# A two-layer diffusion backbone on one core: the context's output projection behind the last tokens, its norm last

## The chip, the cores and the metric

The kernel runs on one core of a Trainium2 chip. The time is the device time of one execution, in microseconds; three runs of the kernel before are given. The engines are PE (TensorE, the matmuls; its weight loads are listed as PEld), DVE (VectorE), ACT (ScalarE), POOL (GpSimd) and SP (SyncE, which issues most of the DMA). Each takes its instructions strictly in the order in which they were placed on it, and they wait for each other by semaphores.

## The reference

Two layers over 1024 latent tokens of width 1024, with 256 context tokens that have the same weights and a conditioning of their own. Cut to what the change touches:

```python
for i in range(2):
    h_lat = rms_norm(x_lat, norm_g[i]) * (1 + sc_l) + sh_l
    h_ctx = rms_norm(x_ctx, norm_g[i]) * (1 + sc_c) + sh_c
    # layer 0: two kinds of attention, heads gated by silu, then @ w_out, for latent and context
    # layer 1: convolution module and neighbourhood attention, for latent tokens only;
    #          of the context it uses keys and values (h_ctx @ w_in)
    x_lat = x_lat + g_l * y_lat
    if i == 0:
        x_ctx = x_ctx + g_c * y_ctx
return rms_norm(x_lat, final_g)
```

Between the layers, then, each token's row of `x` gets the output projection of layer 0 added, is normalised by its root mean square, scaled and shifted, and is the input of layer 1's projections.

## The kernel before

All numbers are float32. A matmul on full precision is made of three: both operands are split into a rounded part (`hh`, `wh`) and the rest (`hl`, `wl`), and `mm3` adds hi·hi, hi·lo and lo·hi into one bank. ScalarE rounds (line 312) and GpSimd or VectorE subtracts (line 315).

Tokens are worked on in three chunks: c = 0 is the context (256 tokens), c = 1 the first 512 latent tokens, c = 2 the last 512. Activations lie transposed: 128 partitions of the width by the tokens of the chunk, eight such tiles (e or dk, 0 to 7).

The program is written as generators that yield between steps. `weave` runs the attention's steps and, after each so many of them, some steps of a second generator as a filling. That gives a program order. The sequence on each engine is then made by a scheduler, which simulates the program with time estimates of its own and prefers what comes earlier in the program order; `tc.issue_after(x)` forbids it to place what is written inside ahead of instruction x. Nothing at run time changes the sequence.

The end of layer 0 is this:

- The attention's last groups: scores (lines 509, 513), exponentials on ScalarE (521), splitting into `ph` and `pl` (312, 315), weighted sums of the values in the bank `ov` (460 to 462), and then, on VectorE, the division by the sum of weights (470 to 473, 670) and the gate (672). Two sets of `ov` follow one another in the same bank.
- `final_proj(c)`: the last quarter of layer 0's output projection for chunk c. For each e, six matmuls (two weight tiles, three each) into a bank `po`, then on VectorE `x += g * po` (line 954), then on ScalarE the square of `x` (979 for the first, 985 after), and an addition of the square to a running sum (987), on GpSimd or VectorE; for the context by odd and even e. For the context and chunk 1 the squares have one buffer, so a square waits until the one before has been added. Chunks 1 and 2 also store `x` to memory; the context doesn't.
- `norm_h(c)`: `rstd_steps` sums the squares over partitions by matmuls with ones (259, `trs`), adds the epsilon (262, `rbv`), raises to the power -1/2 on GpSimd (246), refines by a Newton step on VectorE (247 to 249, `nt`, `nr`), and, two yields later, spreads the result over the partitions by matmuls with the identity (269, `bc`). `make_h` then multiplies all eight tiles on VectorE (322), shifts on ScalarE (325 or 328) and splits (312; 315 on GpSimd or 326 on VectorE).

In the kernel before, the filling of the attention's last steps is: projection of chunk 1, its norm, projection of the context, its norm. Projection and norm of chunk 2 follow when the attention is done. Layer 1 starts with `conv_proj`: value (first product `p`), gate (second) and a third, of other weights (`od_cs`), for chunk 1 and then for chunk 2; then the convolution on VectorE (1083, 1085) while further projections run on TensorE. At the very end a final norm is made for pieces of the tokens by the same `rstd_steps`; its squares are added on lines 1442 and 1445, and its multiplies are on GpSimd (1458, from a copy of the broadcast made on line 1453) and VectorE (1460).

Of the kernel before, what the change touches and what calls it, by code (L numbers as in the profile page):

```python
# [18 lines left out]
P = 128  # L19
# [49 lines left out]
NFILL = (39, 39, 36)  # L69
GL = 12  # L70
HV = 'gggvvvvg'
O1 = (6, 65, 41, 14)
TICK0, TICK1 = (1, 3)
PLAN = 'p0mmnbwmm1h2nbhnbh'
MWR = "ABxAVx"
# [13 lines left out]
def tile_kernel(ctx: ExitStack, tc: tile.TileContext, a, out):  # L89
    nc = tc.nc  # L90
    VE, SC, GP, PE, SY = nc.vector, nc.scalar, nc.gpsimd, nc.tensor, nc.sync
# [12 lines left out]
    def bank(tag, name):  # L104
        if tag == "pp" and solo[0]:
            turn[0] += 1
            tag = ("pp", "mx")[turn[0] // 2 % 2]
        return ps.tile([P, 512], F32, tag=tag, name=name, bufs=BUFS[tag])
# [3 lines left out]
    def nm(s):  # L112
        uid[0] += 1
        return f"{s}_{uid[0]}"
# [17 lines left out]
    ones = cp.tile([P, 2], F32, tag="ones", name="ones")  # L132
# [109 lines left out]
    def newton_rsqrt(pool, v, n, tag):  # L242

        r = pool.tile([P, 16], F32, tag=tag + "r", name=nm("nr"), bufs=2)
        t = pool.tile([P, 16], F32, tag=tag + "t", name=nm("nt"), bufs=2)
        GP.tensor_tensor(r[:, :n], v, mhalf[:, :n], op=ALU.pow)
        VE.tensor_tensor(t[:, :n], r[:, :n], v, op=ALU.mult)
        VE.scalar_tensor_tensor(t[:, :n], t[:, :n], -0.5, r[:, :n], op0=ALU.mult, op1=ALU.mult)
        VE.scalar_tensor_tensor(r[:, :n], t[:, :n], 1.5, r[:, :n], op0=ALU.add, op1=ALU.mult)
        return r  # L250

    def rstd_steps(pool, accs, n, tag, inv=1.0, tr="tr"):


        nb = n // P
        tr = bank(tr, nm("trs"))
        for b in range(nb):
            for k, acc in enumerate(accs):
                PE.matmul(tr[:, 2 * b : 2 * b + 2], acc[:, b * P : (b + 1) * P], ones, start=(k == 0),
                          stop=(k == len(accs) - 1))  # L260
        v = pool.tile([P, 8], F32, tag="rbv", name=nm("rbv"), bufs=2)
        VE.tensor_scalar(v[:, :nb], tr[:, 0 : 2 * nb].rearrange("p (b two) -> p b two", two=2)[:, :, 0],
                         inv, EPS, op0=ALU.mult, op1=ALU.add)
        r = newton_rsqrt(pool, v[:, :nb], nb, "rb")
        yield
        yield
        bc = bank(tag, nm("bc"))
        for b in range(nb):
            PE.matmul(bc[:, b * P : (b + 1) * P], r[:, b : b + 1].broadcast_to([P, P]), ident, start=True, stop=True)
        return bc  # L270
# [9 lines left out]
    def run(gen):  # L280

        while True:
            try:
                next(gen)
            except StopIteration as e:
                return e.value


    def new_h(c):
        if c == 0:  # L290
            t = bigp.tile([P, 2, DK, 256], F32R, tag="big", name=nm("hc"))
            return (t[:, 0], t[:, 1])
        th = bigp.tile([P, DK, 512], F32R, tag="big", name=nm("hh"))
        tl = bigp.tile([P, DK, 512], F32R, tag="big", name=nm("hl"))
        return (th, tl)
# [32 lines left out]
                SC.activation(x, x, AF.Identity, bias=shift)  # L328
                split(x, h[0][:, dk, :], h[1][:, dk, :])

    def mm3(o, lh, ll, rh, rl, first, last):
        PE.matmul(o, lh, rh, start=first, stop=False)  # L332
        PE.matmul(o, lh, rl, start=False, stop=False)  # L333
        PE.matmul(o, ll, rh, start=False, stop=last)  # L334

    def w_tiles(pool, n, width, bufs, rb):

# [355 lines left out]
    with ExitStack() as p0x:  # L693
# [6 lines left out]
        with tc.tile_pool(name="st0", bufs=1, reuse_waits="tile") as st0:  # L700
# [36 lines left out]
            accs, bcs, mh = [], [], [(0, 0), (0, 1), (1, 0), (1, 1)]  # L737
# [180 lines left out]
    with tc.tile_pool(name="o0", bufs=1, reuse_waits="tile") as op_:  # L918
# [26 lines left out]
        def out0(fs, e, c, wh, wl):  # L945
            n = CHUNKS[c][1]
            es = slice(e % 2 * P, (e % 2 + 1) * P)
            cond = 1 if c == 0 else 0
            pp = bank("pp", nm("po"))
            for f in fs:  # L950
                mm3(pp[:, :n], wh[f][:, es], wl[f][:, es], oh[c][0][:, f, :], oh[c][1][:, f, :], f == fs[0], f == fs[-1])
                if f % 2 == 1:
                    yield
            VE.scalar_tensor_tensor(x1[c][:, e, :], pp[:, :n], modT[0][:, 16 + e, cond : cond + 1], x1[c][:, e, :],  # L954
                                    op0=ALU.mult, op1=ALU.add)

        def out0_part(fs):
            for e2 in range(4):
                w = load_w(op_, a["ev_wo"], e2, 256, WO, dks=fs, rb=2)
                if fs == parts[0]:  # L960
                    load_x1(e2)
                for e in (2 * e2, 2 * e2 + 1):
                    for c in range(3):
                        yield from out0(fs, e, c, *w)

        accs = {}

        def final_proj(c):

            t0, n = CHUNKS[c]  # L970
            na = 2 if c == 2 else 1
            pool, tag, bufs = (kvp, "QH", 3) if c == 2 else (op_, "acc1", 1)
            accs[c] = [pool.tile([P, 512], F32, tag=tag, name=nm("acc1"), bufs=bufs)[:, :n] for _ in range(na)]
            for e in range(DK):
                yield from out0(final, e, c, *ws[e // 2])
                if c > 0:
                    SY.dma_start(X1[:, e, t0 - 256 : t0 - 256 + n], x1[c][:, e, :])
                if e < na:
                    SC.activation(accs[c][e], x1[c][:, e, :], AF.Square)
                else:  # L980
                    if c < 2:
                        sq = op_.tile([P, 512], F32, tag="sq1", name=nm("sq1"), bufs=1)
                    else:
                        sq = kvp.tile([P, 512], F32, tag="QL", name=nm("sq1"), bufs=3)
                    SC.activation(sq[:, :n], x1[c][:, e, :], AF.Square)
                    k = e % na if e < 7 else 0
                    (GP if (k if c == 2 else e % 2) else VE).tensor_tensor(accs[c][k], accs[c][k], sq[:, :n], op=ALU.add)

        def norm_h(c):

            n = CHUNKS[c][1]
            bc = yield from rstd_steps(op_, accs[c], n, "pp", tr="pp")
            h1[c] = new_h(c)
            make_h(1, c, lambda dk: x1[c][:, dk, :], bc[:, :n], h1[c])
            yield

        weave(main, O1[0], load_oh(parts[0]), 6, False)
        weave(main, O1[1], out0_part(parts[0]), 48, False)
        weave(main, O1[2], chain(load_oh(parts[1]), out0_part(parts[1])), 30, False)
        ws = [load_w(op_, a["ev_wo"], e2, 256, WO, "gv"[e2 % 2], dks=final, rb=2) for e2 in range(4)]  # L1000
        fill = chain(final_proj(1), norm_h(1), final_proj(0), norm_h(0))
        weave(main, NSTEP[U1 // 2] - GL - O1[0] - O1[1] - O1[2], fill, O1[3])
        solo[0] = True
        run(final_proj(2))
        run(norm_h(2))
    a0x.close()


# [606 lines left out]
```

## Time and profile before

| | |
|---|---|
| three runs | 1559.18, 1565.87, 1557.75 us (median 1559.18) |
| profiled execution | 1559.91 us; its span 1558.1 us; mean granted clock 0.965 |
| TensorE busy | 1459.1 us, 94% |
| VectorE busy | 1050.0 us, 67% |
| GpSimd busy | 801.5 us, 51% |
| ScalarE busy | 746.9 us, 48% |

The page sums the busy time of each engine over the whole span; a view of windows gives the same for any stretch, with the clock that TensorE was granted there (1.00 is full). A list of groups gives count, busy time, mean duration, and the idle time ahead of such instructions with what ended it. A timeline gives single instructions: start, busy time, engine, line, operation, and in brackets the idle time before them.

### The profile page before, as it was taken

Reading aid. Unit: us, or ns where it says so; the run is one execution under the profiler, and the core shown is the slowest. Engines: PE = TensorE matmul, PEld = TensorE weight load, DVE = VectorE, ACT = ScalarE, POOL = GpSimd, SP = SyncE. Lnnn points to the kernel's source line nnn. Section 1 sums busy time; section 2 is a strip of 40 time slices with the busy share of each in tenths; the row PEclk is TensorE's granted clock in tenths of the full one; section 3 lists DMA queues with packets and bytes.
Section 4 is the critical chain, followed back from the end, with each engine's and each line's share of the span. In section 5 each row is a group of like instructions: output and inputs, shape, how many; then the busy total and the mean of one; then the engine's idle time right before and its main releaser. Section 6 shows DMA issues by size and latency. Waiting matters only on the chain.

```text
span 1558.1 us, 21469 instructions
## 1 busy us (share of the span) xinstructions
PE 1459.1 (94%) x7084; PEld 1175.6 (75%) x7084; DVE 1050.0 (67%) x2113; ACT 746.9 (48%) x1418; POOL 801.5 (51%) x637
## 2 busy tenths in 40 slices
PE   6899999998998989999999878999999899989995
PEld 2786978896896768876866657888887688868875
DVE  2833557579579765466677846999756566577866
ACT  3721434444435564447556663443334355455563
POOL 3530434455445765557656664665632344364675
PEclk9899999999999999999999889999999899999996
DMA  9473315422312245121112012111445777878632
GB/s 366 161 244 124 108 57 181 143 70 92 119 51 79 92 151 177 54 68 50 51 31 92 7 34 86 58 55 41 142 159 192 216 204 236 263 227 243 183 111 108
DMA packets 154168, 199.83 MB, mean 128 GB/s; under 512 B 14716, under 2 KB 95816, under 8 KB 154056
## 3 DMA queue, kind: packets, MB, share of 16 engines
q1 hardware_dynamic: 147392, 186.88, 38.0%
q10 hardware_dynamic: 6664, 11.57, 2.3%
q8 instruction: 56, 0.92, 0.2%
q14 instruction: 56, 0.46, 0.1%
HBM read 148.07 MB, written 49.02 MB: 126 GB/s over the span
## 4 chain that ended last, share of the span: by engine, by line
PE 79%; DVE 13%; DMA 3%; issue 2%; ACT 2%; POOL 1%; SPq 0%; DVEq 0%; POOLq 0%; ACTq 0%
PE p L332 7%; PE p L333 7%; PE p L334 7%; PE ov L460 4%; PE ov L462 4%; PE ov L461 4%; PE st L509 4%; PE st L513 4%; PE po L333 4%; PE po L332 4%; PE po L334 4%; PE pq L332 3%; PE pq L334 3%; PE pq L333 3%; PE pm L184 2%
## 5 line engine op out<-in xcount | busy, mean ns | idle before, releaser
L315 POOL TENSOR_TENSOR pl<-pf,ph 128x512 fp32r<-128x512 f32 (+4 forms) x321 | 396.8, 1247 | 375.8 <-ACT ph L312 328.7
L521 ACT ACTIVATE pf<-st 128x512 f32<-128x512 f32 x284 | 166.3, 597 | 210.3 <-PE st L513 171.0
L315 POOL TENSOR_TENSOR wl<-wr,wh 128x512 fp32r<-128x512 f32 (+2 forms) x131 | 170.5, 1313 | 141.4 <-ACT wh L312 121.4
L312 ACT CAST ph<-pf 128x512 fp32r<-128x512 f32 (+4 forms) x364 | 209.2, 588 | 29.0 <-PE ov L461 16.7
L332 PE MATMUL p<-hh,wh 128*128 128x512 f32 x448 | 178.2, 398 | 5.3 <-ACT hh L312 2.8
L333 PE MATMUL p<-hl,wh 128*128 128x512 f32 x448 | 176.1, 394 | 0.6 <-POOL hl L315 0.6
L334 PE MATMUL p<-hh,wl 128*128 128x512 f32 x448 | 173.7, 394 | 0.0
L509 PE MATMUL st<-QH,KAt 128*128 128x512 f32 (+4 forms) x364 | 140.9, 388 | 8.9 <-ACT pf L521 8.1
L460 PE MATMUL ov<-ph,Vt 128*128 128x512 f32 (+4 forms) x364 | 142.5, 392 | 5.6 <-DVE y L670 4.3
L462 PE MATMUL ov<-pl,Vt 128*128 128x512 f32 (+4 forms) x364 | 141.9, 390 | 1.8 <-POOL pl L315 1.8
L461 PE MATMUL ov<-ph,Vt 128*64 128x512 f32 (+4 forms) x364 | 140.5, 386 | 0.0
L513 PE MATMUL st<-QL,KBt 68*128 68x512 f32 (+4 forms) x364 | 136.4, 386 | 2.0 <-DVE QL L438 2.0
L1085 DVE SCALAR_TENSOR_TENSOR cps<-U,taps,cps 128x512 f32<-128x512 f32 x184 | 126.4, 751 | 0.9
L312 ACT CAST wh<-wr 128x512 fp32r<-128x512 f32 (+2 forms) x134 | 81.2, 613 | 92.3 <-DMA wr<-in_od_d_dram 19.1
L332 PEld LDWEIGHTS p<-hh,wh 128*128 128x128 f32 x448 | 85.1, 190 | 23.8 <-ACT hh L312 3.0
L333 PEld LDWEIGHTS p<-hl,wh 128*128 128x128 f32 x448 | 85.2, 190 | 18.7 <-POOL hl L315 1.7
L334 PEld LDWEIGHTS p<-hh,wl 128*128 128x128 f32 x448 | 85.1, 190 | 17.5
L633 DVE TENSOR_REDUCE mp<-mx 128x1 f32<-128x512 f32 x128 | 85.2, 681 | 17.4 <-PE mx L632 16.5
L332 PE MATMUL pq<-wh,hh 128*128 128x384 f32 x256 | 88.4, 345 | 2.8 <-ACT hh L312 2.8
L509 PEld LDWEIGHTS st<-QH,KAt 128*128 128x128 f32 x364 | 69.7, 192 | 26.5 <-ACT pf L521 11.9
L954 DVE SCALAR_TENSOR_TENSOR x<-po,modT,x 128x512 f32<-128x512 f32 (+1 forms) x72 | 47.0, 657 | 62.1 <-PE po L334 61.7
L333 PE MATMUL pq<-wl,hh 128*128 128x384 f32 x256 | 87.4, 342 | 0.0
(280 smaller groups left out, 3470.8 us busy)
## 6 DMA issues: line engine op xcount, KB each, us to landing
mw<-in_mod_w_dram SPq DMA_DIRECT2D x16, 1024.0 KB, 5.5
Q<-qs SPq DMA_DIRECT2D x40, 256.0 KB, 2.2
QH<-Q SPq DMA_DIRECT2D x80, 128.0 KB, 2.7
mw<-in_mod_w_dram SPq DMA_DIRECT2D x16, 512.0 KB, 6.7
wr<-in_od_d_dram SPq DMA_DIRECT2D x32, 256.0 KB, 3.2
wr<-in_ev_qkv_dram SPq DMA_DIRECT2D x16, 384.0 KB, 5.2
KAt<-KD SPq DMA_DIRECT2D x16, 384.0 KB, 5.9
wr<-in_od_wo_dram SPq DMA_DIRECT2D x22, 256.0 KB, 3.3
```

The costliest lines, as they stand in the source:

```text
L312: acts.append(SC.copy(hi, src))
L315: (GP if leng == "g" else VE).tensor_tensor(lo, src, hi.bitcast(F32), op=ALU.subtract)
L332: PE.matmul(o, lh, rh, start=first, stop=False)
L333: PE.matmul(o, lh, rl, start=False, stop=False)
L334: PE.matmul(o, ll, rh, start=False, stop=last)
L460: PE.matmul(o, V[:, 64:192], ph[:, :n], start=(t == 0), stop=False)
L461: PE.matmul(g.ov[0:64, q0 : q0 + n], V[:, 0:64], ph[:, :n], start=False, stop=False)
L462: PE.matmul(o, V[:, 64:192], pl[:, :n], start=False, stop=(last and g.sink is None))
L509: sts.append(PE.matmul(st[:, :n], KA[:, cs], g.QH[:, q0 : q0 + n], start=True, stop=False))
L513: PE.matmul(st[:, :n], KB[0:68, cs], g.QL[0:68, q0 : q0 + n], start=False, stop=True)
L521: acts.append(SC.activation(pf[:, :n], st[:, :n], AF.Exp, scale=1.0 if g.bias else SCALE))
L1085: VE.scalar_tensor_tensor(pc, uc, w, pc, op0=ALU.mult, op1=ALU.add)
```

## The change

Five places are edited: the number 14 in `O1`, which says how many steps of the filling go with the attention's last steps, is 11; a list `last` collects the last matmul of every `mm3` and the matmuls of `rstd_steps` (the parameter `last` of `mm3` is renamed `end`); the context's projection and norm are taken out of the filling; and behind the projection of chunk 2 they are written out by hand. `pinned(gen, k)` runs k steps of a generator such that nothing in them is placed ahead of the latest matmul in `last`. The order by hand: four steps of the context's projection (four e), the sums of chunk 2's norm, the other four e, broadcast and making of chunk 2's `h`, and then the context's norm. What is computed is the same.

```diff
-O1 = (6, 65, 41, 14)
+O1 = (6, 65, 41, 11)
...
+    last = []
+
     def rstd_steps(pool, accs, n, tag, inv=1.0, tr="tr"):
...
-                PE.matmul(tr[:, 2 * b : 2 * b + 2], acc[:, b * P : (b + 1) * P], ones, start=(k == 0),
-                          stop=(k == len(accs) - 1))
+                last.append(PE.matmul(tr[:, 2 * b : 2 * b + 2], acc[:, b * P : (b + 1) * P], ones, start=(k == 0),
+                                      stop=(k == len(accs) - 1)))
...
-    def mm3(o, lh, ll, rh, rl, first, last):
+    def mm3(o, lh, ll, rh, rl, first, end):
         PE.matmul(o, lh, rh, start=first, stop=False)
         PE.matmul(o, lh, rl, start=False, stop=False)
-        PE.matmul(o, ll, rh, start=False, stop=last)
+        last.append(PE.matmul(o, ll, rh, start=False, stop=end))
...
-        fill = chain(final_proj(1), norm_h(1), final_proj(0), norm_h(0))
+        fill = chain(final_proj(1), norm_h(1))
         weave(main, NSTEP[U1 // 2] - GL - O1[0] - O1[1] - O1[2], fill, O1[3])
         solo[0] = True
         run(final_proj(2))
-        run(norm_h(2))
+        f0, n2 = final_proj(0), norm_h(2)
+
+        def pinned(gen, k):
+            with tc.issue_after(last[-1].ins):
+                for _ in range(k):
+                    next(gen, None)
+
+        pinned(f0, 4)
+        pinned(n2, 1)
+        pinned(f0, 5)
+        next(n2)
+        pinned(n2, 2)
+        run(norm_h(0))
```

In the changed kernel line numbers from 261 on are 2 higher, and from the end of layer 0 on 14 higher.

On TensorE the context's matmuls leave the attention's last steps and come in two halves around the sums of chunk 2. Here is the changed kernel's TensorE where the projection of chunk 2 ends and layer 1 begins (`po` are banks of the projection, `hc` the context's operand, `hh` the latent tokens', `trs` and `bc` sums and broadcast of a norm, `p_2417` the value, `p_2418` the gate):

```order
L336 MATMUL po_9362<-hh_7170,wl_8824 128x512
L334 MATMUL po_9375<-hc_7129,wh_8805 128x256
...
L336 MATMUL po_9406<-hc_7129,wl_8812 128x256
L261 MATMUL trs_9413<-ones,acc_2347_9280 128x2
...
L334 MATMUL po_9434<-hc_7129,wh_8817 128x256
...
L271 MATMUL bc_9478<-ident,nr_9424 128x128 x4
L334 MATMUL p_2417_9654<-hh_9225,wh_9607 128x512
...
L261 MATMUL trs_9513<-ones,acc_2363_9374 128x2 x2
L334 MATMUL p_2418_9679<-hh_9225,wh_9607 128x512
```

Before, the sums of chunk 2 came behind the product `p` that is first here, and its broadcast behind the second; now the first comes behind the broadcast, and 24 context matmuls stand on each side of the sums.

On VectorE, the division of the last but one set of weighted sums (`ov`, reciprocal `r`, quotient `y`) stood among the context's norm before (`x_1769` is the context's `x`):

```order
L249 SCALAR_TENSOR_TENSOR nr_9356<-nt_9357,nr_9356 128x2
L322 SCALAR_TENSOR_TENSOR x_1769_7130<-x_1769_7130,gs_105,bc_9362 128x256 x8
L470 STREAM_TRANSPOSE r_2306_9123<-ov_8931 64x256 x2
L326 SCALAR_TENSOR_TENSOR hc_9365<-x_1769_7130,modT_103,hc_9365 128x256
L472 RECIPROCAL r_2307_9124<-r_2306_9123 128x8
L326 SCALAR_TENSOR_TENSOR hc_9365<-x_1769_7130,modT_103,hc_9365 128x256
L473 STREAM_TRANSPOSE rb_9125<-r_2307_9124 128x256
L670 TENSOR_TENSOR y_9130<-ov_8931,rb_9125 64x256 x2
```

and now stands alone:

```order
L317 TENSOR_TENSOR pl_8989<-pf_8990,ph_8988 128x512
L472 STREAM_TRANSPOSE r_2299_9093<-ov_8931 64x256 x2
L474 RECIPROCAL r_2300_9094<-r_2299_9093 128x8
L475 STREAM_TRANSPOSE rb_9095<-r_2300_9094 128x256
L672 TENSOR_TENSOR y_9100<-ov_8931,rb_9095 64x256 x2
```

The context's norm is now on VectorE behind chunk 2's, ahead of the first instruction of the convolution.

The scheduler also sorts some steps of layer 1 anew, though nothing is edited there. The place that the prediction speaks of is GpSimd at the end of the program (`sq` are squares of the final norm, `nr_15684` and `nr_15779` the powers of its last two pieces, `bcs` the copied broadcasts). Before:

```order
L1442 TENSOR_TENSOR sq_3810_15698<-sq_3810_15698,sq_3822_15744 128x256
L246 TENSOR_TENSOR nr_15684<-rbv_15682,mhalf 128x2
L246 TENSOR_TENSOR nr_15779<-rbv_15777,mhalf 128x2
L1458 TENSOR_TENSOR x_3242_13685<-x_3242_13685,bcs_15756 128x256 x4
L1458 TENSOR_TENSOR x_3242_13685<-x_3242_13685,bcs_15788 128x256
```

Now:

```order
L246 TENSOR_TENSOR nr_15684<-rbv_15682,mhalf 128x2
L1456 TENSOR_TENSOR sq_3810_15698<-sq_3810_15698,sq_3822_15744 128x256
L1472 TENSOR_TENSOR x_3242_13685<-x_3242_13685,bcs_15756 128x256 x4
L246 TENSOR_TENSOR nr_15779<-rbv_15777,mhalf 128x2
L1472 TENSOR_TENSOR x_3242_13685<-x_3242_13685,bcs_15788 128x256
```

The last piece's power has four multiplies of the piece before it ahead of it. Its broadcast on TensorE is still the last one.

## The prediction

> **What bounds the kernel now.** I read the shares and the chain of waits first, then windows around the change, then groups and single instructions in them.
>
> ```profile
> span 1558.1 us, 21469 instructions
> PE 1459.1 (94%) x7084; PEld 1175.6 (75%) x7084; DVE 1050.0 (67%) x2113; ACT 746.9 (48%) x1418; POOL 801.5 (51%) x637
> PE 79%; DVE 13%; DMA 3%; issue 2%; ACT 2%; POOL 1%; SPq 0%; DVEq 0%; POOLq 0%; ACTq 0%
> ```
>
> TensorE is busy 94% of the span and makes 79% of the chain: an edit pays only where TensorE idles or runs at a lower clock. The change touches 869 to 967 us, so here is that stretch by stage: second-last attention group (869 to 892), last group (892 to 907), the handover to its weighted sums (907 to 911), these sums (911 to 924), their division (924 to 927), the projection of the last tokens (927 to 941), layer 1's first projection (941 to 954), and the wait for its second token chunk (954 to 967). The columns are TensorE, its weight loads, VectorE, ScalarE and GpSimd busy, the granted clock, and DMA. The last row, from a second query, is a sample of the convolution that follows.
>
> ```profile
> 869.00:892.00 23.00, 19.30 (x103) 13.88 (x100) 22.69 (x38) 16.37 (x32) 18.22 (x14) 1.00 0.00 1
> 892.00:907.00 15.00, 12.42 (x53) 8.25 (x53) 10.81 (x21) 11.40 (x25) 10.92 (x11) 1.00 0.03 9
> 907.00:911.00 4.00, 0.92 (x3) 0.51 (x4) 3.87 (x9) 3.55 (x9) 3.71 (x4) 0.79 0.00 0
> 911.00:924.00 13.00, 12.18 (x40) 8.16 (x40) 2.88 (x6) 8.35 (x15) 8.74 (x8) 0.80 0.11 40
> 924.00:927.00 3.00, 0.00 (x0) 0.00 (x0) 2.46 (x7) 0.34 (x2) 0.00 (x0) 0.90 0.00 0
> 927.00:941.00 14.00, 13.88 (x49) 11.18 (x50) 7.46 (x10) 6.22 (x12) 7.73 (x6) 0.78 0.53 174
> 941.00:954.00 13.00, 13.00 (x68) 11.07 (x67) 2.69 (x7) 1.06 (x3) 1.41 (x2) 1.00 0.17 61
> 954.00:967.00 13.00, 9.44 (x31) 6.64 (x30) 11.95 (x15) 7.82 (x14) 5.58 (x12) 0.74 0.06 20
> 1040.00:1060.00 20.00, 20.00 (x90) 16.56 (x89) 18.89 (x30) 9.37 (x13) 11.69 (x9) 1.00 0.17 53
> ```
>
> So the bound changes: VectorE in 869 to 892 (22.69 of 23), nobody alone in 892 to 907, VectorE again with TensorE nearly empty in 907 to 911, TensorE at a clock of 0.80 after that hole, then TensorE to 954, and VectorE's norm chain in 954 to 967. From 980 on TensorE is full (20.00 of 20) with VectorE close behind (18.89).
>
> **The change, part one: the context leaves the attention.** In 869 to 892 the context's projection costs VectorE these two groups:
>
> ```profile
> L954 DVE SCALAR_TENSOR_TENSOR x<-po,modT,x 128x256 f32<-128x256 f32 x8 | 3.6, 467 | 0.0
> L987 DVE TENSOR_TENSOR acc<-acc,sq 128x256 f32<-128x256 f32 x2 | 1.5, 748 | 0.0
> ```
>
> VectorE sets that stretch, so all of 3.6 + 1.5 = 5.1 us should come back: 3.6 at least (the adds might fall into VectorE's new waits), 5.4 at most (23.00 less the 17.6 that VectorE then has left). TensorE's work there shrinks too and doesn't bind: 19.30 less the 48 context matmuls.
>
> In 892 to 907 TensorE idles 2.58 of 15 us; some of it is the context's adds and norm on GpSimd, ScalarE and VectorE. The view doesn't say how much: 0 to 2.6; I take 1.2, about half.
>
> In 903 to 911 the context's norm stands on VectorE ahead of the attention's division, which stays:
>
> ```profile
> L326 DVE SCALAR_TENSOR_TENSOR hc<-x,modT,hc 128x256 fp32r<-128x256 f32 x4 | 3.3, 831 | 0.1
> L322 DVE SCALAR_TENSOR_TENSOR x<-x,gs,bc 128x256 f32<-128x256 f32 x8 | 3.2, 476 | 0.8 <-PE bc L269 0.8
> ...
> 906.58 0.92 DVE L470 STREAM_TRANSPOSE r<-ov 64x256 f32<-64x256 f32 x2
> ...
> 904.29 0.40 PE L462 MATMUL ov<-pl,Vt 128*128 128x512 f32 x1
> 910.82 0.77 PE L460 MATMUL ov<-ph,Vt 128*128 128x512 f32 x1 [1.98 <-DVE y L670]
> ...
> 923.21 0.40 PE L462 MATMUL ov<-pl,Vt 128*128 128x512 f32 x1
> ...
> 925.32 0.85 DVE L670 TENSOR_TENSOR y<-ov,rb 64x256 f32<-64x256 f32 x2
> ```
>
> The sums end at 904.29 + 0.40 = 904.69 and the next ones may use their bank at 910.82: 6.1 us. The same chain 20 us later, with nothing in its way, goes from 923.61 to the end of the division at 925.32 + 0.85 = 926.17, in 2.6. That gives 3.5 us. I let it reach from 2.0 (GpSimd's and ScalarE's share of the hole may remain; both were busy over 3.5 of the 4 us) to 4.0.
>
> After the hole the matmuls run slowly:
>
> ```profile
> 911.82 0.63 PE L462 MATMUL ov<-pl,Vt 128*128 128x512 f32 x1
> ...
> 918.69 0.40 PE L509 MATMUL st<-QH,KAt 128*128 128x512 f32 x1
> ```
>
> In this listing the first dozen starts after 911.39 are 0.427 us apart, later ones 0.23: 12 x 0.197 = 2.4 us lost. If the hole shrinks to 2.6 or less, this may go. Holes that were followed by the low clock here are 2.76 us long (before 957.53, below) and the pair before 910.82; the shortest such hole is thus about as long as the one that would remain. I take 1.7, bounds 0 and 2.4.
>
> The Trainium skill ("TensorE: Matmul & The Clock Gate", Part 1, what's actually happening) says that the clock halves after at least one idle window of about 3.4 us that runs freely, whatever the kernel does. This trace agrees with the halving, though holes of 2.76 us sufficed. By that rule alone a hole of 2.6 would never halve the clock and the whole 2.4 would come back, 0.7 more than in my sum.
>
> Sum: 5.1 + 1.2 + 3.5 + 1.7 = **11.5 us earlier** at the end of the attention; bounds 3.6 + 0 + 2.0 + 0 = 5.6 and 5.4 + 2.6 + 4.0 + 2.4 = 14.4.
>
> **Part two: the context comes back behind the last tokens.** Pace of its matmuls, then the present chain at this place:
>
> ```profile
> 876.69 0.28 PE L332 MATMUL po<-hc,wh 128*128 128x256 f32 x1
> 876.81 0.28 PE L333 MATMUL po<-hc,wh 128*128 128x256 f32 x1
> ...
> 947.80 1.84 PE L259 MATMUL trs<-ones,acc 128*128 128x2 f32 x16
> 953.72 1.05 PE L269 MATMUL bc<-ident,nr 128*128 128x128 f32 x8
> 957.53 0.80 PE L332 MATMUL p<-hh,wh 128*128 128x512 f32 x1 [2.76 <-ACT hh L312]
> 958.89 0.79 PE L333 MATMUL p<-hl,wh 128*128 128x512 f32 x1 [0.56 <-POOL hl L315]
> 967.39 0.50 PE L332 MATMUL p<-hh,wh 128*128 128x512 f32 x1 [0.63 <-ACT wh L312]
> ...
> 954.81 5.36 DVE L322 SCALAR_TENSOR_TENSOR x<-x,gs,bc 128x512 f32<-128x512 f32 x8 [3.29 <-PE bc L269]
> 964.99 0.69 DVE L1065 SCALAR_TENSOR_TENSOR U<-thc,p 128x512 f32<-128x512 f32 x1
> ```
>
> I keep the old clock of the trace, with the last tokens done at 941.0. 24 context matmuls at 0.12 apart take 2.9: the norm's sums start at 943.9, not 947.8. The sums take 1.84 as now, and 24 more matmuls 2.9: the broadcast comes at 948.6, its end at 949.6. The steps on VectorE and GpSimd between sums and broadcast take 3.7 (947.80 to the last Newton step at 951.5 in this listing), so they fit if VectorE is free. It isn't quite: the order puts context evictions and three context adds ahead, and these hang on one buffer for the squares. Square (0.41 on ScalarE, row below), add (0.75) and a handover come to some 1.3 us each; six of them from 942.4 end at 950.2, where the norm's first multiply then starts (954.81 now). TensorE's 24 matmuls of the projection (20 us hold 90, so 0.222 each, 5.3) run 949.6 to 954.9. The next 24 wait for the bank of the broadcast, read by eight multiplies (5.36) until 955.6, and end at 960.9. The context's broadcast takes 0.5. The second chunk's operands are ready at 950.2 + (957.53 - 954.81) = 952.9, so its 24 run without the 2.76 and 0.56 of waits and at the full clock, to 966.7. Then TensorE waits for the weights cast on ScalarE, now queued behind the tanh of that product: 968.0 to 968.6, against 967.39. TensorE is 0.6 to 1.2 late. VectorE starts the convolution later: 955.6 + 4.8 of the last tokens' norm, then the context's broadcast at 961.4 and its norm (3.2, and 1.9 to 3.3 for the second group) end at 966.5 to 967.9, against 964.99: 2 late. Both are nearly full in the convolution, so I take **1.6 later**, bounds 1.0 earlier (the holes' slow clock is worth more than the context's matmuls) and 3.0 later (VectorE's 2.9 in full).
>
> No DMA moves with the context: its rows aren't stored here. The convolution weights' load and GpSimd's clearing wait, as now, only for the second chunk's norm.
>
> **Part three: a re-sorted end.** The new order changes the last microseconds, though no line there is edited: the last norm's power on GpSimd now stands behind four multiplies of the norm before.
>
> ```profile
> 1547.96 1.20 PE L269 MATMUL bc<-ident,nr 128*128 128x128 f32 x4
> 1548.38 0.70 POOL L246 TENSOR_TENSOR nr<-rbv,mhalf 128x2 f32<-128x2 f32 x1 [1.90 <-DVE rbv L262]
> 1549.20 0.37 ACT L1453 COPY bcs<-bc 128x256 f32<-128x256 f32 x1 [3.32 <-PE bc L269]
> 1549.60 4.60 DVE L1460 SCALAR_TENSOR_TENSOR x<-x,fg,bc 128x256 f32<-128x256 f32 x11
> 1549.65 3.46 POOL L1458 TENSOR_TENSOR x<-x,bcs 128x256 f32<-128x256 f32 x5 [0.57 <-ACT bcs L1453]
> 1549.72 1.22 PE L269 MATMUL bc<-ident,nr 128*128 128x128 f32 x4 [0.55 <-DVE nr L249]
> ```
>
> Now the power runs at 1548.38 and the seven last multiplies on VectorE end at 1549.60 + 4.60 = 1554.2. In the new order the first broadcast goes ahead of the last sums, some 0.7 earlier (1547.2), its copy ends at 1548.8, four multiplies of 3.46/5 = 0.69 end at 1551.6, power 0.70, Newton 0.6, broadcast 1.2 (to 1554.1), seven multiplies of 0.42: 1557.1. **2.9 later**; bounds 2.0 (copy a microsecond earlier) and 3.5.
>
> Small re-sorting inside layer 1 (attention steps and their loads) touches steps I can't price singly: 0, bounds -2.5 and +2.5 (the largest hole of the stretch above, once).
>
> **Sum.** -11.5 + 1.6 + 2.9 = -7.0. The profiled execution took 1559.91 (span 1558.1, and 1.8 around it): 1552.9. It lies 0.7 above the median 1559.18, so against the median **1552.2 us**. All good ends give -14.4 - 1.0 + 2.0 - 2.5 = -15.9 (1543.3), all bad ones -5.6 + 3.0 + 3.5 + 2.5 = +3.4 (1562.6).
>
> **Rivals.** *Full gain* (chance 0.25): the clock stays full through the last group and every wait there goes. -14.4 - 1.0 + 2.9 = -12.5: 1546.7. For it: VectorE has nothing else in 907 to 911 that the sums need. Against: ScalarE and GpSimd were as full there.
>
> *The gain is eaten in the attention* (0.22): without the context's 48 matmuls, which filled holes, TensorE idles more in 869 to 892, and the clock drops there once (2.4 lost), while 892 to 907 and the slow dozen keep their time: 5.1 + 3.5 - 2.4 = 6.2; -6.2 + 1.6 + 2.9 = -1.7: 1557.5. For it: that stretch had 3.7 us idle even with them. Against: the clock there is 1.00, and the holes are spread.
>
> *The square chain holds the norm* (0.10; slower). In the attention the same one-buffer chain went slowly:
>
> ```profile
> 879.71 0.41 ACT L979 ACTIVATE acc<-x 128x256 f32<-128x256 f32 x1
> ...
> 897.42 0.73 POOL L987 TENSOR_TENSOR acc<-acc,sq 128x256 f32<-128x256 f32 x1 [0.81 <-ACT sq L985]
> ```
>
> From first square to last add 18.4 us. At about that pace (17 from 942) the last tokens' first multiply, behind the chain's sixth add on VectorE, starts at 959.0 instead of 950.2, 8.8 later; TensorE then has a hole of some 9 us and the slow dozen again (2.4): -7.0 + 8.8 + 2.4 = +4.2, 1563.4. It decides once the chain takes 7 us more than my 7.8. Against it: its engines are loaded 2.69, 1.06 and 1.41 of 13 us there.
>
> That the change doesn't do what it says is excluded by the order: the context's matmuls stand on both sides of the sums.
>
> **Chances and range.** Forecast 0.43, full gain 0.25, eaten 0.22, slower rival 0.10. The forecast's own range is 1549 to 1556. Half a per cent, 7.8 us, is about what a measurement of this kernel can tell: faster means below 1551.4, slower above 1567.0. Faster: 0.42 of the forecast (0.18) and nearly all of the full gain (0.24), 0.42. Slower: part of the slow rival and something unforeseen, 0.08. Same: 0.50. The range 1545.5 to 1560.5 takes in the full gain and the eaten one and leaves out the slow rival and the outer ends.
>
> **What would show it.** Right: the windows of the second-last group shorten by 5 us; the wait before the last group's sums is below 3 us and the clock behind it is 1.00; no hole of 2.76 before the second chunk; the last power waits behind GpSimd's four multiplies. Wrong: a granted clock below 0.9 between 869 and 905; VectorE's first multiply of the last norm of layer 0 over 10 us after the last tokens; or a span that differs by over 3 us outside these three places, which would make the re-sorted layer 1 the cause.

## The result

The changed kernel takes 1556.4 us in the median of 22 runs (1553.1 to 1563.0), beside 1561.6 us for the kernel before in the same series (22 runs, 1555.2 to 1567.0). The measured ratio is 0.9973, 95% interval 0.9962 to 0.9983: about 4.2 us faster by the ratio, 5.2 by the two medians, within the half per cent that was called no change. In two later series the same kernel came out at 0.9947 (0.9927 to 0.9967) and 0.9968 (0.9953 to 0.9982) of the kernel before. The forecast was 7.0 us faster. Its level of 1552.2 rested on a median of 1559.18 for the kernel before, 2.4 below the later one.

The page of the changed kernel, its span and its chain of waits by engine:

```profile
span 1555.8 us, 21467 instructions
PE 1462.5 (94%) x7084; PEld 1177.6 (76%) x7084; DVE 1046.0 (67%) x2113; ACT 747.6 (48%) x1418; POOL 800.2 (51%) x637
PE 81%; DVE 11%; DMA 3%; issue 2%; ACT 2%; POOL 1%; SPq 0%; DVEq 0%; POOLq 0%; ACTq 0%
```

Two percentage points of the chain went from VectorE to TensorE, and no other share moved.

The end of the attention, in windows cut by events instead of round numbers: from the broadcast of chunk 1's norm to the last but one set of weighted sums, from there to the last set, and from there to the projection of chunk 2. The kernel before:

```profile
869.30:892.34 23.04, 19.00 (x101) 13.72 (x100) 22.70 (x39) 16.21 (x31) 17.92 (x14) 1.00 0.00 1
892.34:910.82 18.48, 13.17 (x55) 8.55 (x56) 14.20 (x28) 14.95 (x32) 14.44 (x14) 0.96 0.03 8
910.82:927.12 16.30, 12.36 (x41) 8.34 (x41) 5.55 (x13) 8.81 (x17) 8.93 (x8) 0.81 0.09 32
```

and the changed kernel:

```profile
872.25:891.20 18.95, 15.27 (x49) 8.92 (x48) 18.55 (x29) 13.94 (x25) 15.53 (x12) 0.75 0.00 0
891.20:906.88 15.68, 14.46 (x51) 9.98 (x52) 5.38 (x13) 11.50 (x20) 9.52 (x9) 0.86 0.03 9
906.88:921.00 14.12, 10.07 (x40) 6.75 (x40) 5.53 (x11) 8.71 (x16) 8.58 (x7) 0.94 0.12 38
```

The stretches shrink by 4.09, 2.80 and 2.18: 9.07 in all. VectorE's load in the first fell by 22.70 - 18.55 = 4.15, and the stretch with it. The granted clock moved: the kernel before had 1.00, 0.96, 0.81, the changed one 0.75, 0.86, 0.94.

The edges of the second stretch on TensorE of the changed kernel (start, busy, line, operation, idle before):

```profile
892.62 0.63 PE L462 MATMUL ov<-ph,Vt 128*128 128x512 f32 x1
...
903.79 0.39 PE L464 MATMUL ov<-pl,Vt 128*128 128x512 f32 x1
...
906.88 0.47 PE L462 MATMUL ov<-ph,Vt 128*128 128x512 f32 x1 [0.47 <-DVE y L672]
907.66 0.39 PE L462 MATMUL ov<-ph,Vt 128*128 128x512 f32 x1
...
921.00 2.07 PE L334 MATMUL po<-hh,wh 128*128 128x512 f32 x4 [3.51 <-ACT hh L314]
```

From the end of the sums (903.79 + 0.39 = 904.18) to the next set it is 2.70 us, 6.13 before: 3.43 gained. Score matmuls run in this time in both kernels, so TensorE idles 1.2 us of the 2.70 and 4.65 of the 6.13. But from 891.20 to 904.18 it is 12.98 us, beside 12.35 before: nothing gained, 0.6 lost. Its first matmuls take 0.63, the duration of the low clock; the last set's take 0.39 at once. The windows of this part alone, before and then in the changed kernel:

```profile
892.34:904.69 12.35, 11.68 (x51) 7.92 (x51) 8.22 (x15) 9.09 (x19) 9.46 (x9) 1.00 0.04 11
```

```profile
891.20:904.18 12.98, 12.98 (x47) 9.35 (x47) 2.88 (x6) 9.01 (x16) 6.93 (x7) 0.83 0.04 11
```

TensorE's waits are gone (busy 12.98 of 12.98), while its clock is 0.83 instead of 1.00.

The start of layer 1 in the changed kernel, TensorE and then VectorE:

```profile
937.44 1.95 PE L261 MATMUL trs<-ones,acc 128*128 128x2 f32 x16
942.61 1.16 PE L271 MATMUL bc<-ident,nr 128*128 128x128 f32 x8 [0.26 <-DVE nr L249]
956.13 0.50 PE L334 MATMUL p<-hh,wh 128*128 128x512 f32 x1 [0.24 <-ACT thc L1078]
962.84 0.50 PE L334 MATMUL p<-hh,wh 128*128 128x512 f32 x1 [0.98 <-ACT wh L314]
...
943.89 0.42 DVE L989 TENSOR_TENSOR acc<-acc,sq 128x256 f32<-128x256 f32 x1 [0.55 <-ACT sq L987]
944.23 5.35 DVE L324 SCALAR_TENSOR_TENSOR x<-x,gs,bc 128x512 f32<-128x512 f32 x8
...
961.14 0.67 DVE L1079 SCALAR_TENSOR_TENSOR U<-thc,p 128x512 f32<-128x512 f32 x1
```

The hole of 2.76 us is gone. Counted from the first matmul of chunk 2's projection (927.12 before, 921.00 now), TensorE reaches the `od_cs` weights after 41.8 us instead of 40.3, and VectorE the convolution after 40.1 instead of 37.9.

Layer 1 also changed, at a place where no line is edited. TensorE's waits between the two gate products and the attention's first maxima, before and after:

```profile
1201.49 0.47 PE L332 MATMUL p<-hh,wh 128*128 128x512 f32 x1 [1.87 <-DVE spq L1141]
1222.40 0.73 PE L1320 MATMUL mx<-KAt,QH 128*128 128x440 f32 x1 [3.39 <-DVE mp L1321]
```

```profile
1189.12 0.50 PE L334 MATMUL p<-hh,wh 128*128 128x512 f32 x1 [1.38 <-DVE spv L317]
1197.34 0.47 PE L334 MATMUL p<-hh,wh 128*128 128x512 f32 x1 [0.21 <-DVE spq L1155]
1217.30 0.73 PE L1334 MATMUL mx<-KAt,QH 128*128 128x440 f32 x1 [4.95 <-DVE mp L1335]
```

Pairing the instructions of VectorE in the two traces, the changed kernel is 4.54 us ahead at 1185 and 5.97 at 1245: this place gave 1.4. In the second trace of the changed kernel it gave 1.95. That it comes from the new order there is argued from the traces; no run undid it alone.

And the end of the program:

```profile
1541.49 1.22 PE L271 MATMUL bc<-ident,nr 128*128 128x128 f32 x4 [2.39 <-DVE nr L249]
1543.20 2.77 POOL L1472 TENSOR_TENSOR x<-x,bcs 128x256 f32<-128x256 f32 x4 [2.17 <-ACT bcs L1467]
1545.92 0.71 POOL L246 TENSOR_TENSOR nr<-rbv,mhalf 128x2 f32<-128x2 f32 x1
1547.28 1.22 PE L271 MATMUL bc<-ident,nr 128*128 128x128 f32 x4 [3.92 <-DVE nr L249]
1548.94 2.83 DVE L1474 SCALAR_TENSOR_TENSOR x<-x,fg,bc 128x256 f32<-128x256 f32 x7 [1.72 <-ACT bcs L1467]
```

The last power waits for four multiplies, as read from the order, and the last broadcast comes 5.79 us after the one before it, 1.76 in the kernel before.

A table by stage is the fairest comparison, since executions with the same order of instructions differ by several us in the 870 us before the change (see the end). The columns are the time from chunk 1's broadcast to chunk 2's projection, from there to the first sums of the convolution's layer norm, from there to the first sums of the final norm, and from there to the end of the span:

| | attention's end | start of layer 1 | rest of layer 1 | end |
|---|---|---|---|---|
| before | 57.82 | 223.92 | 372.86 | 34.20 |
| before, with its end re-sorted (a run below) | 57.39 | 223.84 | 373.85 | 37.54 |
| changed | 48.75 | 225.50 | 370.95 | 38.35 |
| changed, second trace | 48.12 | 225.37 | 370.64 | 38.12 |
| changed, third trace | 48.53 | 226.11 | 370.67 | 38.11 |

In the mean the change gains 9.35, loses 1.74, gains 2.11 and loses 3.99 against the one trace of the kernel before: 5.7 us in all. The second row has the order of the kernel before in its first three stages and repeats them to 0.4, 0.1 and 1.0 us, and two traces of one kernel below (the whole end put back) have 370.3 and 372.2 in the third, so the 2.11 is known to a microsecond or two.

### The profile page after: what moved, and what is told of

Same layout as the page of the kernel before. It is cut to its first block, busy times and chain, and to the rows that moved or that the text cites. A ratio compares the mean times of both kernels' runs of the same rounds, so it can differ in the third digit from the quotient of the medians.

```text
span 1555.8 us, 21467 instructions
## 1 busy us (share of the span) xinstructions
PE 1462.5 (94%) x7084; PEld 1177.6 (76%) x7084; DVE 1046.0 (67%) x2113; ACT 747.6 (48%) x1418; POOL 800.2 (51%) x637
## 4 chain that ended last, share of the span: by engine, by line
PE 81%; DVE 11%; DMA 3%; issue 2%; ACT 2%; POOL 1%; SPq 0%; DVEq 0%; POOLq 0%; ACTq 0%
PE p L334 7%; PE p L336 7%; PE p L335 7%; PE ov L462 5%; PE ov L464 5%; PE ov L463 4%; PE st L511 4%; PE st L515 4%; PE po L334 4%; PE po L335 4%; PE po L336 4%; PE pq L334 3%; PE pq L335 3%; PE pq L336 3%; PE pg L334 2%
## 5 line engine op out<-in xcount | busy, mean ns | idle before, releaser
L464 PEld LDWEIGHTS ov<-pl,Vt 128*128 128x128 f32 x364 | 71.0, 195 | 23.3 <-POOL pl L317 5.0
```

The costliest lines, as they stand in the source:

```text
L464: PE.matmul(o, V[:, 64:192], pl[:, :n], start=False, stop=(last and g.sink is None))
```

## The experiments

**The changed kernel again**, in two further series.

> The changed kernel once more, for a second trace of the same program. Theory: the attention's end gains about 9.5 us, the start of layer 1 gives 2 back and the last norm another 3 to 4, so it is 3 to 6 us faster than the kernel before. If the low clock in the second-last attention group belongs to the new order, the granted clock between the broadcast of chunk 1's norm and the last group's first weighted sum is again below 0.9; if it was chance, it is 1.00 this time and the stretch is about 17.6 us instead of 18.95.

It took 0.9947 (0.9927 to 0.9967) of the kernel before, in five runs: 8.3 us faster by the ratio, more than the 3 to 6 expected. The first stretch was 18.94 us, the second 15.07, with six slow matmuls behind 887.59 instead of nine, and the clock was low again:

```profile
878.00:887.00 9.00, 6.51 (x14) 3.34 (x14) 8.89 (x13) 6.21 (x12) 8.88 (x7) 0.63 0.00 0
```

So the low clock belongs to the order, while its length varies. All eight traces in which the context leaves the attention and no filling is put in its place show it at the first matmuls of the last group.

> The changed kernel beside its version with the old end, on one chip, since the two were timed on different chips so far. Theory by the stages of the traces (attention 9.1 to 9.8 earlier, start of layer 1 1.6 later, a re-sorted place in layer 1 1.4 to 2 earlier, end 4.0 later): 5 to 6 us faster than the kernel before.

0.9968 (0.9953 to 0.9982), 1556.5 beside 1561.0 us: 5.0 us by the ratio and 4.6 by the medians, at the lower end of the 5 to 6 expected. Its stages are in the table.

**The end put back, first attempt.** The last norm's power and Newton steps are placed ahead of the multiplies of the piece before.

```diff
-EVS = "e1 c1 e2 f1 c2 f2".split()
+EVS = "e1 c1 e2 c2 f1 f2".split()
...
-        GP.tensor_tensor(r[:, :n], v, mhalf[:, :n], op=ALU.pow)
+        pows.append(GP.tensor_tensor(r[:, :n], v, mhalf[:, :n], op=ALU.pow))
...
-        VE.scalar_tensor_tensor(r[:, :n], t[:, :n], 1.5, r[:, :n], op0=ALU.add, op1=ALU.mult)
+        pows.append(VE.scalar_tensor_tensor(r[:, :n], t[:, :n], 1.5, r[:, :n], op0=ALU.add, op1=ALU.mult))
...
-                    yield from final_norm(k, bcs[k])
+                    with tc.issue_after(pows[-2].ins), tc.issue_after(pows[-1].ins):
+                        yield from final_norm(k, bcs[k])
```

> The change, with the end of the program put back: the last norm's power and Newton steps stand ahead of the multiplies of the piece before it, on GpSimd and VectorE. Theory (the re-sorted end costs 3 to 4 us): 3 to 4 us faster than the changed kernel, about 1552.5, 0.994 to 0.996 of the kernel before. Rival (the end is set by the output transfers, and the late power is hidden): within 1 us of the changed kernel.

It missed: 1556.4 us, ratio 0.9972 (0.9958 to 0.9985), no faster than the change. The trace says why; TensorE, GpSimd and VectorE between the two last broadcasts:

```profile
1542.36 0.85 PE L263 MATMUL trs<-ones,sq 128*128 128x2 f32 x4
1543.49 0.71 POOL L248 TENSOR_TENSOR nr<-rbv,mhalf 128x2 f32<-128x2 f32 x1 [2.60 <-DVE rbv L266]
1544.17 2.77 POOL L1474 TENSOR_TENSOR x<-x,bcs 128x256 f32<-128x256 f32 x4
1544.23 0.68 DVE L249 TENSOR_TENSOR nt<-nr,rbv 128x2 f32<-128x2 f32 x1 [0.82 <-POOL nr L248]
1544.94 0.65 DVE L250 SCALAR_TENSOR_TENSOR nt<-nt,nr 128x2 f32<-128x2 f32 x1
1546.33 1.22 PE L273 MATMUL bc<-ident,nr 128*128 128x128 f32 x4 [3.11 <-DVE nr L251]
```

The power runs at 1543.49 now and not behind the multiplies, but the last piece's sums still stand behind the other piece's broadcast (1541.35), because their additions on GpSimd and VectorE are late too. And the Newton steps, 0.16 us each where GpSimd doesn't work beside them (at 1540.94 and 1541.13 in this trace), take 0.65 to 0.68 while it multiplies. The Trainium skill ("GPSIMD Engine Reference", 1. Specifications) says that GpSimd's interfaces to SBUF are shared with VectorE, with contention for instructions with two SBUF inputs; these rows, 0.16 against 0.68, agree. The two last broadcasts are 4.98 apart, where the change has 5.79 and the kernel before 1.76: 0.8 of four microseconds was undone, and by the last stage (37.73) about half a microsecond.

**The whole end put back.** Both additions on GpSimd stand ahead of both powers, the sums ahead of the broadcast, the multiplies behind both Newton steps.

```diff
-EVS = "e1 c1 e2 f1 c2 f2".split()
+EVS = "e1 e2 z1".split()
...
+                if ev[0] == "z":
+                    s1, s2 = (rstd_steps(dpool, sums[j], ENDS[j][2], BCT[j]) for j in (1, 2))
+                    with tc.issue_after(adds[0].ins), tc.issue_after(adds[1].ins):
+                        next(s1)
+                    next(s2)
+                    with tc.issue_after(last[-1].ins):
+                        bcs[1], bcs[2] = run(s1), run(s2)
+                    with tc.issue_after(pows[-2].ins), tc.issue_after(pows[-1].ins):
+                        yield from final_norm(1, bcs[1])
+                    yield from final_norm(2, bcs[2])
```

(`adds` holds the last additions of squares on GpSimd and on VectorE, `pows` the powers and last Newton steps as above.)

> The change, with the whole end in the order of the kernel before: both additions of squares on GpSimd ahead of both powers, the last piece's sums on TensorE ahead of the other piece's broadcast, all multiplies behind both Newton steps. Theory (the re-sorted end costs 4 us, and the first attempt kept 3 of them because sums, additions and broadcast stayed late): the last broadcast comes about 26 us after the first sums of the final norm, as in the kernel before, instead of 29.8; 3 to 4 us faster than the changed kernel, ratio to before 0.992 to 0.995. Rival (the output transfers set the end): as the changed kernel.

1551.7 us, ratio 0.9946 (0.9927 to 0.9965). The last broadcasts follow each other without a gap, here eight matmuls as one row:

```profile
1537.71 1.01 PE L263 MATMUL trs<-ones,sq 128*128 128x2 f32 x4 [2.39 <-DVE rbv L266]
1539.08 2.47 PE L273 MATMUL bc<-ident,nr 128*128 128x128 f32 x8 [0.36 <-DVE nr L251]
```

The last stage of the table is 35.4 us, beside 38.1 to 38.4 in the change and 34.2 before: 2.8 of the 4.0 came back.

> The change with the whole end in the old order, beside the change. Theory: 3.5 to 4 us faster than the change, 9 to 10 faster than the kernel before (ratio 0.994). Rival (the first comparison was luck of the low clock elsewhere in the program, which moves single executions by several us): within 1.5 us of the change.

0.9942 (0.9921 to 0.9964), 1553.6 us, 2.9 less than the change beside it (1556.5); its last stage is again 35.4. Of both kernels and all the versions tried this has the lowest ratios, 8.4 and 9.1 us below the kernel before. Against the change itself the intervals still overlap, so that it is faster than the change rests on the last stage of the traces.

**Only the end, on the kernel before.**

```diff
-                    bcs[k] = yield from rstd_steps(dpool, sums[k], ENDS[k][2], BCT[k])
+                    if k == 2:
+                        st_ = rstd_steps(dpool, sums[k], ENDS[k][2], BCT[k])
+                        with tc.issue_after(muls[-1].ins):
+                            next(st_)
+                        bcs[k] = yield from st_
+                    else:
+                        bcs[k] = yield from rstd_steps(dpool, sums[k], ENDS[k][2], BCT[k])
```

(`muls` holds GpSimd's multiplies of the final norm.)

> The kernel before, with only the end re-sorted: the last norm's power behind four multiplies on GpSimd. Theory: 2.5 to 4 us slower than the kernel before, ratio 1.0016 to 1.0026. Rival (hidden by the output transfers): within 1 us.

1564.9 us, ratio 1.0023 (1.0009 to 1.0037), 3.6 us slower, and 3.3 by the last stage (37.54 against 34.20). The late power alone costs that: the sums and additions of the last piece still stand ahead of the other piece's broadcast here.

```profile
1548.82 1.20 PE L269 MATMUL bc<-ident,nr 128*128 128x128 f32 x4
1553.24 0.70 POOL L246 TENSOR_TENSOR nr<-rbv,mhalf 128x2 f32<-128x2 f32 x1
1554.58 1.22 PE L269 MATMUL bc<-ident,nr 128*128 128x128 f32 x4 [4.56 <-DVE nr L249]
```

**Only the context's norm last**, its projection still in the attention.

```diff
-        fill = chain(final_proj(1), norm_h(1))
+        fill = chain(final_proj(1), norm_h(1), final_proj(0))
...
-        f0, n2 = final_proj(0), norm_h(2)
+        n2 = norm_h(2)
...
-        pinned(f0, 4)
-        pinned(n2, 1)
-        pinned(f0, 5)
-        next(n2)
-        pinned(n2, 2)
+        run(n2)
         run(norm_h(0))
```

(`O1[3]` is 14 again.)

> Half of the change: the context's projection stays in the attention, only its norm comes last, behind that of chunk 2. Theory: the second-last attention group keeps its 23 us (evictions and adds still on VectorE), the hole before the last weighted sums closes from 6.1 to about 2.7 us, the last group from its first sums to the next projection takes 14.1 instead of 16.3: 5 to 6 us earlier at the end of the attention. The start of layer 1 has no context matmuls to fill the norm's wait, so TensorE idles there and gives back 3 to 6. Total within 2 us of the kernel before on one side, 4 faster at best. Rival (the context's projection causes the hole, not its norm): the hole stays at 6 us.

0.9992 (0.9974 to 1.0010): no change. Its attention splits the gain; chunk 1's broadcast stands at 875.11 in this trace, the projection of chunk 2 at 927.18:

```profile
898.14 0.55 PE L462 MATMUL ov<-ph,Vt 128*128 128x512 f32 x1 [1.41 <-DVE y L672]
899.34 0.63 PE L462 MATMUL ov<-ph,Vt 128*128 128x512 f32 x1
...
913.08 0.47 PE L462 MATMUL ov<-ph,Vt 128*128 128x512 f32 x1 [0.44 <-DVE y L672]
```

23.03, 14.94 and 14.10 us. So the projection's evictions and adds are worth the 4.1 of the first stretch, and the norm the 5.7 of the other two, of which the whole change got 5.0 to 5.6. The clock was low behind 898.14 here too, for some nine matmuls, though the context's matmuls were still in the attention: that they are gone is thus not the only thing that lets it fall there. The start of layer 1 cost 1.5, less than expected, and the end stayed re-sorted (36.4).

**Without the interleaving**, the context's projection whole ahead of the sums or whole behind the broadcast.

```diff
-        pinned(f0, 4)
+        pinned(f0, 9)
         pinned(n2, 1)
-        pinned(f0, 5)
         next(n2)
         pinned(n2, 2)
```

> The change without its interleaving: all eight steps of the context's projection ahead of the sums of chunk 2's norm. Theory: attention as in the change; TensorE has nothing left to fill the norm's 3.7 us between sums and broadcast except layer 1's first product, and the first multiply of the norm comes 2 to 3 us later than in the change: 1 to 3 us slower than the change. The power of the last norm stands ahead of the multiplies here, which by the run before is worth 1. Rival (the interleaving brings nothing, since TensorE is late by the context's matmuls either way): the same time as the change.

0.9973 (0.9958 to 0.9989). TensorE waits 2.46 for the norm, the first product of layer 1 stands behind the broadcast, and the start of layer 1 takes 229.0 us, 3.3 more than in the change. The total is the change's all the same because the end came out in another order and took 35.0 us, 3.2 less:

```profile
943.61 2.07 PE L271 MATMUL bc<-ident,nr 128*128 128x128 f32 x8 [2.46 <-DVE nr L249]
```

```diff
-        pinned(f0, 4)
         pinned(n2, 1)
-        pinned(f0, 5)
         next(n2)
         pinned(n2, 2)
+        pinned(f0, 9)
         run(norm_h(0))
```

> The change without its interleaving, the other way: the context's projection behind the broadcast of chunk 2's norm. Theory: attention as in the change; TensorE has only layer 1's first product between the sums and the broadcast, and the context's matmuls fill the wait for chunk 2's operands, but their evictions queue on VectorE behind the norm's 8 multiplies and splits, so the context's norm and with it the convolution on VectorE begin 3 to 5 us later: 2 to 4 us slower than the change. Rival (VectorE has slack there): the same time.

1.0047 (1.0033 to 1.0061), 6.6 us slower than the kernel before by the medians; the start of layer 1 takes 239.7 us, 14 more than in the change, and more than the 2 to 4 expected. The edit did not put all of the projection behind the broadcast: the scheduler set 18 of the 48 matmuls ahead of it, while the norm's steps ran. Behind it TensorE itself stops for VectorE twice among the context's matmuls, first until the last of the norm's eight multiplies is done, then for an eviction that queues behind the norm's splits. These stops are 6.9 of the 14; the rest was not taken apart.

```profile
946.25 0.36 PE L334 MATMUL po<-hc,wh 128*128 128x256 f32 x1 [4.10 <-DVE x L324]
951.30 0.58 PE L334 MATMUL po<-hc,wh 128*128 128x256 f32 x1 [2.77 <-DVE x L956]
```

**TensorE kept busy in the attention.** Context matmuls whose sums nobody reads stay in the attention; first all 48 as a plain filling, then 42 placed by hand into the holes of the first stretch.

```diff
+        def warm():
+            for e in range(DK):
+                pp = bank("pp", nm("po"))
+                for f in final:
+                    es = slice(e % 2 * P, (e % 2 + 1) * P)
+                    wh, wl = ws[e // 2]
+                    mm3(pp[:, :256], wh[f][:, es], wl[f][:, es], oh[0][0][:, f, :], oh[0][1][:, f, :], f == final[0], f == final[-1])
+                    if f % 2 == 1:
+                        yield
+
-        fill = chain(final_proj(1), norm_h(1))
+        fill = chain(final_proj(1), norm_h(1), warm())
```

(`O1[3]` is 14 again.)

> The change, with the 48 context matmuls also left in the attention where they were, their result read by nobody: TensorE gets the same filling as before, VectorE, ScalarE and GpSimd don't. Theory (the missing filling lets TensorE's clock drop between 880 and 895, and that ate 2 us of the gain): clock 1.00 there, the stretch from the norm's broadcast to the last group's sums 17.5 to 18 us instead of 18.95 and the next one 14.5 instead of 15.7: 2 us faster than the changed kernel. Rival (VectorE sets the stretch whatever the clock): no change, or up to 2 us slower, since TensorE has 5.8 us more to do.

0.9974 (0.9958 to 0.9989). The first stretch had the full clock and still took 19.41 us, with VectorE as busy as before, so VectorE sets it, and the theory that the clock ate that gain fell:

```profile
868.01:887.42 19.41, 17.08 (x100) 13.82 (x98) 19.07 (x29) 14.62 (x26) 16.93 (x12) 0.99 0.01 1
887.42:902.05 14.63, 13.40 (x50) 9.18 (x50) 6.26 (x13) 11.13 (x20) 9.56 (x8) 0.90 0.03 9
```

The filling ran early, and the clock dropped behind it, at 887. The total says nothing about the filling: the scheduler sorted layer 1 anew again, and its start took 229.0 us and its rest 374.0, both over 3 us more than in the change.

> The change with the old end and 42 context matmuls whose result nobody reads, placed by hand in TensorE's holes of the second-last attention group (between 878 and 891 of the changed kernel's trace), where the first such filling ran too early. Theory (the clock, low for 6 to 10 matmuls in all traces of the change, costs the first part of the last group 0.2 us for each): no slow matmul behind the last group's first weighted sum, that part 11.1 to 11.6 us instead of 12.3 to 13.0; the group before it stays at 18.9 to 19.4, since VectorE sets it; about 1 us faster than the change with the old end, which a time can hardly tell. Rival (GpSimd and ScalarE set the pace there): 12.3 us even at the full clock.

```diff
-            for e in range(DK):
+            b = len(sts)
+            for e, j in enumerate((19, 19, 18, 18, 17, 16, 16)):
+                with tc.issue_after(sts[b - j].ins):
...
```

(This is the second filling, against the first; `sts` lists the attention's score matmuls, `O1[3]` is 11, and the end is in the old order.) 0.9951 (0.9931 to 0.9970). The part from the first set of sums took 10.45 us at the full clock, less than the 11.1 to 11.6 expected:

```profile
894.45:904.90 10.45, 10.45 (x46) 7.58 (x44) 2.37 (x5) 8.75 (x16) 6.95 (x6) 1.00 0.04 13
```

But the filling was itself too much. The clock fell within the first stretch instead (matmuls of 0.63 us from 885.70 to 890.40), that stretch took 21.63 us, and from broadcast to last set it is 34.78 us, beside 33.90 to 34.67 in the eight traces of this order without filling. So the filling that lifts the clock costs what it brings.

The traces side by side say more about this part. TensorE is busy in it without a gap each time, and the part is longest at the lowest clock and shortest at the full one: 12.98 us at 0.83, 12.37 at 0.88 (the second trace of the change), 11.93 at 0.87 (the first filling), 10.45 at 1.00. That speaks for the clock as what kept the gain of the last group from showing. Whether ScalarE and GpSimd would have kept up at the full clock without the longer stretch ahead of it isn't shown.

## Why the prediction was wrong, and where it was right

The forecast was -11.5 + 1.6 + 2.9 = -7.0. The traces show -9.35 + 1.74 + 3.99 and, in the rest of layer 1 that was put at 0, -2.11: -5.7; the first series gave -4.2. The step that failed is the first sum, the 11.5 us at the end of the attention, which measured 9.35, and within it two terms; then the size of the end. The three steps fell short by 3.4 us together, and the 2.1 in a place that nobody priced hid most of it: that the total lies only 1.3 from the forecast is luck. Of the signs of being wrong that the prediction named, one came: the granted clock below 0.9 between 869 and 905 (0.75 and 0.86 in the first two stretches).

- *5.1 in the second-last group*: 4.1. VectorE does set this stretch (the full clock changed nothing), but one of the two adds that were counted lies behind the division that ends it, and the splits beside the removed work take 0.4 us longer (5.41 instead of 4.99). The row of the prediction had taken in both adds; this one, in the kernel before, starts when the division has ended:

```profile
892.23 0.43 DVE L987 TENSOR_TENSOR acc<-acc,sq 128x256 f32<-128x256 f32 x1
```

- *1.2 in the last group*: none, -0.6 to 0.0 in the three traces. The waits that the term was made of did go, but the step let the clock stay at 1.00, and it was 0.83 to 0.88: it falls in the second-last group and is still low for six to nine matmuls here. The rival "eaten in the attention" named this drop and gave it 2.4 us; the mechanism was there each time, its price was about this term. That the clock is the cause is argued from the traces side by side (above), not shown by a run that changes it alone.
- *3.5 at the hole*: 3.43, and the row in which the undisturbed chain took 2.6 was the right one to read: it is 2.70 now. *1.7 of slow matmuls behind it*: 2.18, and no slow matmul was left. By the rule of the Trainium skill ("TensorE: Matmul & The Clock Gate", Part 1, what's actually happening) that the prediction cites, the whole 2.4 was to come back, nearer than the middle that was taken. The "hole" of this term was read too long, though: with the score matmuls in it TensorE idled 1.2 us, not 2.7.
- *1.6 at the start of layer 1*: 1.45 to 2.19. The norm's first multiply, forecast 23.1 us behind chunk 2's first matmul, came after 23.2; TensorE's loss of 0.6 to 1.2 was 1.6, VectorE's 2 was 2.3. The rival of the square chain fell: the last add ends at 944.3, and the multiply follows without a wait.
- *2.9 at the end*: 4.0, beyond the upper bound of 3.5. The mechanism is right (the kernel before with the late power alone lost 3.6, by its last stage 3.3), and so is its wait: the last two broadcasts were to be 5.7 us apart and are 5.8. What failed is that the first of them was to come 0.7 earlier: counted from the first sums of the final norm it comes after 23.8 to 24.0 us, 24.1 before. The last multiplies were to end 4.2 us behind the start of the last broadcast, and end after 4.5, as before. The late sums and additions that the first attempt at undoing laid bare cost nothing of their own as long as the power is late: with the power alone moved the two broadcasts are 5.76 apart.
- *0 for the re-sorted rest*: -2.1, inside its bounds.
- The chances: within half a per cent, at 0.50, was the likeliest class and came.

## What to carry to other kernels

Where a scheduler sorts the program, an edit in one place moves instructions in others; here these gained 2 us and lost 4, beside 7.6 gained by the edit itself, and 2.8 of the 4 could be had back by writing the order down. Price what an engine does up to the instruction that ends the stretch, not up to a round number. Work taken from a matmul engine can come back as a lower clock one stage later.

## What the runs showed that was not expected

The clock fell without any long hole. In the changed kernel the longest idle time of TensorE ahead of the first slow matmuls is 1.12 us, from 880.45 to 881.57:

```profile
879.18 0.50 PE L464 MATMUL ov<-pl,Vt 128*128 128x512 f32 x1 [0.26 <-POOL pl L317]
879.51 0.94 PE L634 MATMUL mx<-KAt,QH 128*128 128x512 f32 x2
881.57 0.57 PE L634 MATMUL mx<-KAt,QH 128*128 128x512 f32 x1 [1.12 <-DVE mp L635]
882.18 0.80 PE L462 MATMUL ov<-ph,Vt 128*128 128x512 f32 x1
```

Of the 3.4 us before 881.57 it idled some 1.4, and the matmuls from 882.18 take 0.63 and more. The Trainium skill ("TensorE: Matmul & The Clock Gate", Part 1, what's actually happening) gives an idle window of about 3.4 us as the condition; a wholly idle one was not needed here. The 2.70 us between two sets in the next group, of which TensorE idled 1.2, had no such effect.

Executions with nearly the same order of instructions up to chunk 1's broadcast reached it between 867.6 and 875.1 us after their start, over thirteen traces, and the difference between two of them arises in steps of 1 to 4 us at single places. That is as much as the whole change, and why single profiles were compared by stage here.
